# The last stage of a decoder trunk: spreading a per-token factor from its column instead of a diagonal, in another order, with stores from two engines

## The chip, the cores and the metric

The kernel runs on one core of a Trainium2 chip. The metric is the device time of one execution in microseconds. A core has five engines that run side by side and meet by semaphores: TensorE (PE; its weight loads are listed as PEld), VectorE (DVE), ScalarE (ACT), GpSimd (POOL) and SyncE (SP). Each takes its own instructions in the order of the program. Transfers between the chip's memory and a core's on-chip memory are started by an engine's queue and carried out by 16 DMA engines.

## The reference

One layer of a hybrid decoder trunk on 264 tokens (256 of a prompt and 8 of a sample), with 2048 features, in float32. After three gated branches and an output projection comes a channel mixer and then the final norm; only the end matters here:

```python
hid = jnp.square(jax.nn.relu(rms_norm(x, g_mlp) @ w_up))
x = x + hid @ w_down                     # 8192 -> 2048
...
y = xf * lax.rsqrt(jnp.mean(xf * xf, axis=-1, keepdims=True) + EPS) * g_final   # rms_norm(x, g_final)
```

The last norm needs, for each token, the sum of the squares of all its 2048 features; no output element can be finished before the last column of `hid @ w_down` is in that sum.

## The kernel before, in words

**Up to the tail.** Features lie on the 128 partitions, tokens along them, so a tensor `X` of 2048 features by 264 tokens is 16 tiles of 128 x 264. Weights come in chunks of 1 MB pairs and are split in two float32r parts, so that each product is three matmuls (lines 192 to 194). A table of chunks (`weight_plan`) sets the order; the work of the other engines is fitted in by a small planner with credits per engine. It ends with the loop over the chunks at line 1023. What follows, from line 1026 on, is written out by hand: the order of the calls is the order in which each engine takes its instructions, and semaphores are added for what depends on what.

**The tail.** Of the last product, 12 of the 16 feature tiles (`KA`) are complete by then and lie in `X`, already scaled by -0.5 times `g_final`, with the sum of their squares, element by element over tiles, in `sq2`. The last 512 features lack only the last four of the 64 contraction tiles. These four are computed the other way round: tokens on the partitions, features along them. For that the 264 tokens are cut into three groups of 128, 96 and 40 (`CUT`). For each group g:

- `half_mm(g, h)`: 12 matmuls (four contraction tiles by three parts) into one PSUM bank, for half h of the 512 features (line 1041). TensorE takes the halves in the order (0,0), (0,1), (1,0), (1,1), (2,0), (2,1).
- `other(g)`: the sum over features of `sq2`, by a matmul with a column of ones, into column g of the PSUM tile `inv` (line 1044). `other_in` reads it and adds the epsilon (line 1054).
- `half_sum(g, h)`: adds the residual on VectorE (line 1058), takes the squares and their sum on ScalarE (line 1062), and weighs by `g_final` on GpSimd (line 1066).
- `mean` twice on VectorE (line 1072): adds the sums of the two halves and the other features, over 2048. The result m stands in column 4 of the small tile `stat`, one row for each token.
- `seed` on ScalarE (line 1069): a first value s of 1/sqrt(m), from a table. One Newton step makes it exact: s (m s s - 3), times the -0.5 in the weights. `stat` column 5 is m s s (line 1078), column 6 the factor (line 1083, `root`).
- `token_out(g)`: scales the group's rows of 512 features by column 6 on ScalarE (line 1088) and stores them to `t_dram` (line 1089).
- The other 12 tiles have the tokens along the partitions, so the factor is needed there as a row, the same in all 128 partitions. `root_diag(g)` makes a diagonal matrix of the factors: the unit matrix times s on ScalarE (line 1077), then (-3 + m s s) times that on VectorE (line 1079). `spread_mm(g)` multiplies it by a matrix of ones: ones as the stationary operand, the diagonal as the moving one (line 1048). This gives the factors along the row in every partition.
- `piece(g, a, b)`: tiles a to b of `X` times that row, on VectorE from PSUM, or on GpSimd from a copy that ScalarE makes (`factor_copy`, line 1092), and a store to `y_dram` (lines 1099 and 1102).

All stores are issued by SyncE, in the order of the calls. The program ends when the last has landed.

Of the kernel before, what the change touches and what calls it, by code (L numbers as in the profile page):

```python
# [12 lines left out]
AF = mybir.ActivationFunctionType  # L13
ALU = mybir.AluOpType
AX = mybir.AxisListType

P = 128
# [3 lines left out]
N = TP + TS  # L21
# [37 lines left out]
PAD = 288  # L59
# [32 lines left out]
def hybrid_step(ctx: ExitStack, tc: tile.TileContext, head_in, x_in, par_in, st_in, row_in, wall, y_out, t_out, st_out):  # L92
    nc = tc.nc
# [34 lines left out]
    def acc():  # L128
        return psum.tile([P, 512], F32, name="acc", tag="acc")

    Gf = G.rearrange("p a n -> p (a n)")
# [82 lines left out]
    def later(n, fn):  # L214
        delayed.append((now[0] + n, fn))
# [263 lines left out]
    def lru_tail():  # L479
# [45 lines left out]
        stage("lru", "act", 0.52, [lambda ct=ct: decay(ct) for ct in range(8)])  # L525
        stage("lru", "pool", 0.2, [reset])
        stage("lru", "act", 0.65, [lambda c=c: root(c) for c in c4])
        stage("lru", "dve", 0.75, [lambda c=c: wide(c, TM, TM) for c in c4], 0)
        stage("lru", "dve", 0.43, [lambda c=c: a_of(c) for c in c4], 0)
# [329 lines left out]
    T = {}  # L859

    def end_tiles():
        e = [cpool.tile([P, 8, N], F32, name=f"end{i}", tag=f"B{i}").rearrange("p a n -> p (a n)") for i in range(4)]
        T["held"] = e[0][:, :4 * PAD].rearrange("p (m n) -> p m n", m=4)
        T["turned"] = e[1][:, :4 * PAD].rearrange("p (m n) -> p m n", m=4)
        T["resid"], T["sum"] = (t[:, :3 * 512].rearrange("p (g n) -> p g n", g=3) for t in e[2:])
        T["unit"], T["eye"] = (e[0][:, 4 * PAD + i * P:4 * PAD + (i + 1) * P] for i in range(2))
        T["minus"] = e[1][:, 4 * PAD + 24 + N:4 * PAD + 24 + N + P]
        nc.gpsimd.memset(T["minus"], -3.0)  # L868
        T["g"] = e[0][:, 4 * PAD + 2 * P:4 * PAD + 2 * P + 512]
        T["stat"] = e[1][:, 4 * PAD:4 * PAD + 24].rearrange("p (k g) -> p k g", g=3)  # L870
        T["copy"] = e[1][:, 4 * PAD + 24:4 * PAD + 24 + N]
        nc.gpsimd.memset(T["held"][:, :, N:], 0.0)
        nc.gpsimd.memset(T["unit"], 1.0)
        nc.gpsimd.affine_select(out=T["eye"], in_=T["unit"], pattern=[[1, P]], compare_op=ALU.is_equal, fill=0.0,
                                base=0, channel_multiplier=-1)
        nc.sync.dma_start(T["g"], row_in)
        later(2, lambda: nc.scalar.activation(T["g"], T["g"], AF.Copy, scale=-0.5))
# [79 lines left out]
    for i, ch in enumerate(chunks):  # L957
# [18 lines left out]
        if kind == "dense":  # L976
            rhs, fn = group(gi)
            n = groups[gi][2] // 2
# [3 lines left out]
            if c == 0:  # L982
                pss = [acc() for _ in range(4)] if gi > 2 else pair[4 * gi - 4:4 * gi]
                if groups[gi][:2] == ("w_down", 48) and groups[gi][3] == 3:
                    end_tiles()
# [40 lines left out]
    nL = len(chunks)  # L1026
    V, U = T["sum"], first[:, :3 * 512].rearrange("p (g n) -> p g n", g=3)
    Y = raw.rearrange("p a c -> p (a c)")
    stat, inv, fb, diag = T["stat"], acc(), [], []
    size = [b - a for a, b in zip(CUT, CUT[1:])]  # L1030

    def toks(g):
        return slice(CUT[g], CUT[g + 1])

    def token_mm(g, ps, a, b, steps):
        for s in steps:
            kt, way = divmod(s, 3)
            slot, at = (nL - 2 + kt // 2) % NHI, kt % 2 * 512
            w = (wlo if way == 2 else whi)[:, slot, at + a:at + b]
            x = hid(3, KD - TAIL + kt)[way == 1]  # L1040
            nc.tensor.matmul(ps[:size[g], :b - a], x[:, toks(g)], sent(w), start=s == 0, stop=s == 3 * TAIL - 1)  # L1041

    def other(g):
        nc.tensor.matmul(inv[:size[g], g:g + 1], sq2[:, toks(g)], ones[:, 0:1], start=True, stop=True)

    def spread_mm(g):
        fb.append(acc())
        nc.tensor.matmul(fb[g][:, :size[g]], T["unit"][:size[g], :], diag[g], start=True, stop=True)  # L1048

    def st_col(k, g):  # L1050
        return stat[:size[g], k, g:g + 1]

    def other_in(a, b):
        nc.vector.tensor_scalar(stat[:size[a], 0, a:b], inv[:size[a], a:b], EPS, None, op0=ALU.add)

    def token_sum(g, ps, a, b):
        n = size[g]
        nc.vector.tensor_tensor(halves(V[:n, g, a:b]), halves(T["resid"][:n, g, a:b]),
                                ps[:n, :b - a].rearrange("p (j t) -> p t j", t=2), op=ALU.add)

    def token_square(g, a, b, k):
        nc.scalar.activation(Gf[:size[g], a:b], V[:size[g], g, a:b], AF.Square, accum_out=st_col(k, g))

    def weighed(g, a, b):
        n = size[g]
        nc.gpsimd.tensor_tensor(U[:n, g, a:b], V[:n, g, a:b], T["g"][:n, a:b], op=ALU.mult)

    def seed(g, k, more):
        nc.scalar.activation(st_col(3, g), st_col(k, g), AF.Abs_reciprocal_sqrt, bias=st_col(more, g), scale=1.0 / D)  # L1069

    def mean(g, k, more, to):
        nc.vector.tensor_scalar(st_col(to, g), st_col(k, g), 1.0 / D, st_col(more, g), op0=ALU.mult, op1=ALU.add)

    def root_diag(g):
        n, y = size[g], st_col(3, g)
        seeded, d = (Gf[:n, (4 + 4 * i) * N + P * g:(4 + 4 * i) * N + P * g + n] for i in range(2))
        nc.scalar.activation(seeded, T["eye"][:n, :n], AF.Copy, scale=y)  # L1077
        nc.vector.scalar_tensor_tensor(st_col(5, g), st_col(4, g), y, y, op0=ALU.mult, op1=ALU.mult)
        nc.vector.scalar_tensor_tensor(d, T["minus"][:n, :n], st_col(5, g), seeded, op0=ALU.add, op1=ALU.mult)  # L1079
        diag.append(d)  # L1080

    def root(g):
        nc.vector.scalar_tensor_tensor(st_col(6, g), st_col(5, g), -3.0, st_col(3, g), op0=ALU.add, op1=ALU.mult)

    def token_out(g):
        n = size[g]
        y = Y[:n, KA * N + 512 * g:KA * N + 512 * (g + 1)]
        nc.scalar.activation(y, U[:n, g, :], AF.Copy, scale=st_col(6, g))
        nc.sync.dma_start(t_out[toks(g), :], y)

    def factor_copy(g):
        nc.scalar.copy(T["copy"][:, toks(g)], fb[g][:, :size[g]])

    def piece(g, a, b, own=False):
        n = size[g]
        at = KA * CUT[g]
        y = Y[:, at + a * n:at + b * n]
        by = T["copy"][:, toks(g)] if own else fb[g][:, :n]
        (nc.gpsimd if own else nc.vector).tensor_tensor(  # L1099
            y.rearrange("p (k n) -> p k n", n=n), X[:, a:b, toks(g)],  # L1100
            by[:, None, :].to_broadcast([P, b - a, n]), op=ALU.mult)
        send = lambda: nc.sync.dma_start(y_out[:, at + a * n:at + b * n], y)
        return send if own else send()

    every = range(3 * TAIL)
    bank = [[acc(), acc()] for _ in range(2)]

    def half_mm(g, h, steps=every):
        token_mm(g, bank[g][h], 256 * h, 256 * h + 256, steps)

    def half_sum(g, h):
        token_sum(g, bank[g][h], 256 * h, 256 * h + 256)
        token_square(g, 256 * h, 256 * h + 256, 1 + 6 * h)
        weighed(g, 256 * h, 256 * h + 256)

    def close(g):
        seed(g, 7, 2)
        mean(g, 7, 2, 4)
        root_diag(g)

    nc.vector.memset(inv[:, 0:3], 0.0)
    half_mm(0, 0)
    half_mm(0, 1)
    other(0)
    half_mm(1, 0)
    other(1)
    other(2)
    half_mm(1, 1, every[:5])
    half_sum(0, 0)
    half_sum(0, 1)  # L1130
    other_in(0, 1)
    mean(0, 1, 0, 2)
    close(0)
    spread_mm(0)
    half_mm(1, 1, every[5:])
    root(0)
    other_in(1, 3)
    token_out(0)
    half_sum(1, 0)
    piece(0, 0, 4)  # L1140
    factor_copy(0)
    send = piece(0, 8, 12, True)
    half_sum(1, 1)
    piece(0, 4, 8)
    send()
    bank.append([acc(), acc()])
    half_mm(2, 0)
    half_sum(2, 0)
    mean(1, 1, 0, 2)
    close(1)  # L1150
    half_mm(2, 1)
    spread_mm(1)
    half_sum(2, 1)
    piece(1, 0, 4)
    root(1)
    mean(2, 1, 0, 2)
    close(2)
    factor_copy(1)
    token_out(1)
    send = piece(1, 9, 12, True)  # L1160
    spread_mm(2)
    root(2)
    piece(1, 4, 9)
    send()
    token_out(2)
    piece(2, 0, 6)
    piece(2, 6, 12)


def _vec(a):  # L1170
# [95 lines left out]
```

## Time and profile before

| what | us |
|---|---|
| median of 3 runs (1302.89 to 1303.65) | 1303.21 |
| the profiled execution | 1303.09 |
| its span, first to last instruction | 1301.4 |
| TensorE busy | 1290.4 |
| VectorE busy | 838.2 |
| ScalarE busy | 722.0 |
| GpSimd busy | 113.3 |
| first matmul of the tail starts at | 1281.55 |
| last matmul of `half_mm(2, 1)` starts at | 1291.60 |
| last product on VectorE starts at | 1296.01 |
| last store is issued at | 1297.83 |

A row of the timeline has the start in us from the span's start, the duration in us, the engine, the line of the kernel, the operation, what is written and read, the shapes, the count, and in brackets how long the engine was idle before and whom it waited for. `end` is the tile that holds `stat`, the residual, the sums, the unit matrix and the copy; `acc` is any PSUM tile; `G` is a scratch tile with the diagonals; `raw` holds the finished output; `first` the weighed rows. SPq, DVEq and the like are an engine's sequencer. A matmul's duration overlaps the next one's. A float32 matmul in `other` or `spread_mm` shows as two instructions of each kind. In the table of windows the columns are the window, its length, the busy time and count of instructions of PE, PEld, DVE, ACT and POOL, the granted clock of TensorE, the share of the 16 DMA engines' time, and GB/s.

### The profile page before, as it was taken

Reading aid. Unit: us, or ns where it says so; the run is one execution under the profiler, and the core shown is the slowest. Engines: PE = TensorE matmul, PEld = TensorE weight load, DVE = VectorE, ACT = ScalarE, POOL = GpSimd, SP = SyncE. Lnnn points to the kernel's source line nnn. Section 1 sums busy time; section 2 is a strip of 40 time slices with the busy share of each in tenths; the row PEclk is TensorE's granted clock in tenths of the full one; section 3 lists DMA queues with packets and bytes.
Section 4 is the critical chain, followed back from the end, with each engine's and each line's share of the span. In section 5 each row is a group of like instructions: output and inputs, shape, how many; then the busy total and the mean of one; then the engine's idle time right before and its main releaser. Section 6 shows DMA issues by size and latency. Waiting matters only on the chain.

```text
span 1301.4 us, 26869 instructions
## 1 busy us (share of the span) xinstructions
PE 1290.4 (99%) x11458; PEld 1289.3 (99%) x11458; DVE 838.2 (64%) x1076; ACT 722.0 (55%) x1036; POOL 113.3 (9%) x154
## 2 busy tenths in 40 slices
PE   9999999999999999999999999999999999999996
PEld 9999999999999999999999999999999999999996
DVE  7886898776776677666555545554555554555554
ACT  7767677667674655455544334543345533455454
POOL 0250010110102023131000000000000000000023
PEclk9999999999999999999999999999999999999999
DMA  9655556555575564656555555555555555555661
GB/s 353 211 180 200 196 201 205 197 196 198 197 228 194 179 212 163 232 184 207 197 196 195 195 195 194 195 195 194 194 195 194 195 194 195 194 195 194 206 208 68
DMA packets 44361, 257.76 MB, mean 198 GB/s; under 512 B 9162, under 2 KB 10186, under 8 KB 15314
## 3 DMA queue, kind: packets, MB, share of 16 engines
q1 hardware_dynamic: 44242, 256.06, 58.2%
q8 instruction: 89, 1.46, 0.4%
q14 instruction: 30, 0.25, 0.1%
HBM read 252.29 MB, written 3.21 MB: 196 GB/s over the span
## 4 chain that ended last, share of the span: by engine, by line
PE 98%; DMA 0%; DVE 0%; ACT 0%; issue 0%; SPq 0%; DVEq 0%; ACTq 0%
PE acc L194 32%; PE acc L192 32%; PE acc L193 32%; PE acc L935 1%; PE acc L1041 0%; DMA first<-head_dram 0%; DVE raw L1099 0%; PE acc L1048 0%; SPq L158 0%; ACT end L1069 0%; ACT G L1077 0%; DVE G L1079 0%; ACT whi L169 0%; ACT A L291 0%; PE acc L266 0%
## 5 line engine op out<-in xcount | busy, mean ns | idle before, releaser
L170 DVE TENSOR_TENSOR wlo<-raw,whi 128x1024 fp32r<-128x1024 f32 (+1 forms) x479 | 586.8, 1227 | 440.6 <-ACT whi L169 434.9
L169 ACT CAST whi<-raw 128x1024 fp32r<-128x1024 f32 (+1 forms) x479 | 493.6, 1033 | 526.7 <-PE acc L193 475.1
L194 PE MATMUL acc<-A,wlo 128*128 128x264 f32 x1952 | 539.7, 276 | 0.0
L192 PE MATMUL acc<-A,whi 128*128 128x264 f32 x1952 | 539.7, 276 | 0.0
L193 PE MATMUL acc<-A,whi 128*128 128x264 f32 x1952 | 539.6, 276 | 0.0
L194 PEld LDWEIGHTS acc<-A,wlo 128*128 128x128 f32 x1952 | 369.5, 189 | 0.0
L192 PEld LDWEIGHTS acc<-A,whi 128*128 128x128 f32 x1952 | 369.5, 189 | 0.0
L193 PEld LDWEIGHTS acc<-A,whi 128*128 128x128 f32 x1952 | 369.5, 189 | 0.0
L194 PE MATMUL acc<-xn,wlo 128*128 128x264 f32 x1024 | 283.1, 276 | 0.0
L193 PE MATMUL acc<-xn,whi 128*128 128x264 f32 x1024 | 283.1, 276 | 0.0
L192 PE MATMUL acc<-xn,whi 128*128 128x264 f32 x1024 | 283.1, 276 | 0.0
L194 PEld LDWEIGHTS acc<-xn,wlo 128*128 128x128 f32 x1024 | 193.9, 189 | 0.0
L192 PEld LDWEIGHTS acc<-xn,whi 128*128 128x128 f32 x1024 | 193.8, 189 | 0.0
L193 PEld LDWEIGHTS acc<-xn,whi 128*128 128x128 f32 x1024 | 193.8, 189 | 0.0
L193 PE MATMUL acc<-Q,whi 128*128 128x264 f32 x628 | 173.6, 276 | 0.0
L192 PE MATMUL acc<-LH,whi 128*128 128x264 f32 x624 | 172.5, 276 | 0.0
L194 PE MATMUL acc<-LH,wlo 128*128 128x264 f32 x624 | 172.5, 276 | 0.0
L193 PEld LDWEIGHTS acc<-Q,whi 128*128 128x128 f32 x628 | 118.9, 189 | 0.0
L192 PEld LDWEIGHTS acc<-LH,whi 128*128 128x128 f32 x624 | 118.1, 189 | 0.0
L194 PEld LDWEIGHTS acc<-LH,wlo 128*128 128x128 f32 x624 | 118.1, 189 | 0.0
L583 ACT ACTIVATE G<-tmp,par 128x256 f32<-128x256 f32 x120 | 54.1, 498 | 2.9 <-DVE G L586 2.1
L868 POOL MEMSET end<- 128x128 f32 x1 | 0.2, 204 | 598.3 <-PE acc L194 598.3
(206 smaller groups left out, 871.7 us busy)
## 6 DMA issues: line engine op xcount, KB each, us to landing
raw<-wall_dram SPq DMA_DIRECT2D x226, 1024.0 KB, 4.9
raw<-wall_dram SPq DMA_DIRECT2D x18, 512.0 KB, 5.6
raw<-wall_dram SPq DMA_DIRECT2D x5, 256.0 KB, 3.3
X<-x_dram SPq DMA_DIRECT2D x4, 264.0 KB, 8.7
so_dram<-st SPq DMA_DIRECT2D x1, 1018.0 KB, 9.5
st<-st_dram SPq DMA_DIRECT2D x1, 912.0 KB
y_dram<-raw SPq DMA_DIRECT2D x3, 256.0 KB, 2.1
X<-x_dram SPq DMA_DIRECT2D x1, 528.0 KB
```

What stands on the lines that cost most here:

```text
L169: nc.scalar.copy(h[:, s], r)
L170: nc.vector.tensor_tensor(lo[:, s], r, f(h[:, s]), op=ALU.subtract)
L192: nc.tensor.matmul(ps[:, :N], whi_t, xh, start=first, stop=False)
L193: nc.tensor.matmul(ps[:, :N], whi_t, xl, start=False, stop=False)
L194: nc.tensor.matmul(ps[:, :N], wlo_t, xh, start=False, stop=last)
L583: nc.scalar.activation(dst[:, ct, :TP], vext[:, ct, k:k + TP], AF.Copy, scale=par[:, w:w + 1])
L868: nc.gpsimd.memset(T["minus"], -3.0)
L935: nc.tensor.matmul(pair[m][:, :N], w[:, m * P:(m + 1) * P], sent(A[:, x, :]), start=start and k == 0, stop=False)
```

## The change

**The spread.** The diagonal is gone, with the constant -3 matrix `T["minus"]` and its memset. `root_diag` becomes `root`, which computes columns 5 and 6 of `stat` only. `spread_mm` now takes column 6 itself, repeated 128 times by a step of zero, as the stationary operand, and the unit matrix as the moving one; the product is the same row in every partition.

**The order.** The first group's part up to `close(0)` now stands ahead of `half_mm(1, 0)`, `other(1)` and `other(2)`; `spread_mm(0)` comes after four steps of `half_mm(1, 1)` instead of five. `other_in(1, 3)` is behind the first piece of group 0. Group 1's first `mean` and its `seed` stand ahead of `half_sum(2, 0)`, and its `token_out(1)` right after its `root`.

**The stores.** `token_out` of groups 0 and 2 is issued by ScalarE, that of group 1 by SyncE. Group 1's GpSimd piece is stored by ScalarE. Group 2's product is one piece of 12 tiles with one store instead of two of six.

```diff
-        T["minus"] = e[1][:, 4 * PAD + 24 + N:4 * PAD + 24 + N + P]
-        nc.gpsimd.memset(T["minus"], -3.0)
...
     def spread_mm(g):
         fb.append(acc())
-        nc.tensor.matmul(fb[g][:, :size[g]], T["unit"][:size[g], :], diag[g], start=True, stop=True)
+        nc.tensor.matmul(fb[g][:, :size[g]], st_col(6, g).to_broadcast([size[g], P]), T["eye"][:size[g], :size[g]],
+                         start=True, stop=True)
...
-    def root_diag(g):
-        n, y = size[g], st_col(3, g)
-        seeded, d = (Gf[:n, (4 + 4 * i) * N + P * g:(4 + 4 * i) * N + P * g + n] for i in range(2))
-        nc.scalar.activation(seeded, T["eye"][:n, :n], AF.Copy, scale=y)
+    def root(g):
+        y = st_col(3, g)
         nc.vector.scalar_tensor_tensor(st_col(5, g), st_col(4, g), y, y, op0=ALU.mult, op1=ALU.mult)
-        nc.vector.scalar_tensor_tensor(d, T["minus"][:n, :n], st_col(5, g), seeded, op0=ALU.add, op1=ALU.mult)
-        diag.append(d)
-
-    def root(g):
-        nc.vector.scalar_tensor_tensor(st_col(6, g), st_col(5, g), -3.0, st_col(3, g), op0=ALU.add, op1=ALU.mult)
+        nc.vector.scalar_tensor_tensor(st_col(6, g), st_col(5, g), -3.0, y, op0=ALU.add, op1=ALU.mult)
...
-        nc.sync.dma_start(t_out[toks(g), :], y)
+        (nc.sync if g == 1 else nc.scalar).dma_start(t_out[toks(g), :], y)
...
-        send = lambda: nc.sync.dma_start(y_out[:, at + a * n:at + b * n], y)
-        return send if own else send()
+        return lambda queue: queue.dma_start(y_out[:, at + a * n:at + b * n], y)
...
     def close(g):
         seed(g, 7, 2)
         mean(g, 7, 2, 4)
-        root_diag(g)
+        root(g)
...
     half_mm(0, 1)
     other(0)
-    half_mm(1, 0)
-    other(1)
-    other(2)
-    half_mm(1, 1, every[:5])
     half_sum(0, 0)
     half_sum(0, 1)
     other_in(0, 1)
     mean(0, 1, 0, 2)
     close(0)
+    half_mm(1, 0)
+    other(1)
+    other(2)
+    half_mm(1, 1, every[:4])
     spread_mm(0)
-    half_mm(1, 1, every[5:])
-    root(0)
-    other_in(1, 3)
+    half_mm(1, 1, every[4:])
     token_out(0)
     half_sum(1, 0)
-    piece(0, 0, 4)
+    piece(0, 0, 4)(nc.sync)
+    other_in(1, 3)
     factor_copy(0)
     send = piece(0, 8, 12, True)
     half_sum(1, 1)
-    piece(0, 4, 8)
-    send()
+    piece(0, 4, 8)(nc.sync)
+    send(nc.sync)
     bank.append([acc(), acc()])
     half_mm(2, 0)
+    mean(1, 1, 0, 2)
+    seed(1, 7, 2)
     half_sum(2, 0)
-    mean(1, 1, 0, 2)
-    close(1)
+    mean(1, 7, 2, 4)
+    root(1)
+    token_out(1)
     half_mm(2, 1)
     spread_mm(1)
     half_sum(2, 1)
-    piece(1, 0, 4)
-    root(1)
+    piece(1, 0, 4)(nc.sync)
     mean(2, 1, 0, 2)
     close(2)
     factor_copy(1)
-    token_out(1)
     send = piece(1, 9, 12, True)
     spread_mm(2)
-    root(2)
-    piece(1, 4, 9)
-    send()
+    piece(1, 4, 9)(nc.sync)
     token_out(2)
-    piece(2, 0, 6)
-    piece(2, 6, 12)
+    send(nc.scalar)
+    piece(2, 0, 12)(nc.sync)
```

More of the change, by code (lines that the diff above doesn't have):

```diff
@@ L1028, in hybrid_step @@
     Y = raw.rearrange("p a c -> p (a c)")
-    stat, inv, fb, diag = T["stat"], acc(), [], []
+    stat, inv, fb = T["stat"], acc(), []
     size = [b - a for a, b in zip(CUT, CUT[1:])]
```

## The prediction

> **What bounds the kernel now.** I read the page first.
>
> ```profile
> span 1301.4 us, 26869 instructions
> PE 1290.4 (99%) x11458; PEld 1289.3 (99%) x11458; DVE 838.2 (64%) x1076; ACT 722.0 (55%) x1036; POOL 113.3 (9%) x154
> L868 POOL MEMSET end<- 128x128 f32 x1 | 0.2, 204 | 598.3 <-PE acc L194 598.3
> ```
>
> TensorE is full for all but some 11 us, and the diff touches nothing ahead of the tail except the removed memset: 0.2 us on an engine that stood idle for 598. So only the tail, from 1282 us on, can move. I read it next in the chain of waits in order of time, then instruction by instruction. TensorE, its weight load (PEld) and VectorE (DVE) in the first group:
>
> ```profile
> 1285.90 0.27 PE acc L1044 x4
> 1284.43 0.42 DVE L1058 TENSOR_TENSOR end<-end,acc 128x256 f32<-128x256 f32 x1 [0.92 <-PE acc L1041]
> 1286.19 0.16 DVE L1054 TENSOR_SCALAR end<-acc 128x1 f32<-128x1 f32 x1 [1.34 <-PE acc L1044]
> 1286.46 0.21 DVE L1072 TENSOR_SCALAR end<-end 128x1 f32<-128x1 f32 x1
> 1286.78 0.21 DVE L1072 TENSOR_SCALAR end<-end 128x1 f32<-128x1 f32 x1
> 1287.11 0.22 DVE L1078 SCALAR_TENSOR_TENSOR end<-end 128x1 f32<-128x1 f32 x1
> 1287.53 0.35 DVE L1079 SCALAR_TENSOR_TENSOR G<-end,G 128x128 f32<-128x128 f32 x1 [0.20 <-ACT G L1077]
> 1287.80 0.15 DVE L1083 SCALAR_TENSOR_TENSOR end<-end 128x1 f32<-128x1 f32 x1
> 1286.60 0.27 PE L1041 MATMUL acc<-whi,Q 128*96 128x256 f32 x1
> 1288.00 0.19 PEld L1048 LDWEIGHTS acc<-G,end 128*128 128x128 f32 x1 [1.34 <-issue]
> 1288.03 0.46 PE L1048 MATMUL acc<-G,end 128*128 128x128 f32 x2 [1.15 <-DVE end L1054]
> 1289.09 0.27 PE L1041 MATMUL acc<-whi,LH 128*40 128x256 f32 x1
> ```
>
> L1054 reads the first group's other sums, but waits until the last of the three groups' L1044 matmuls ends at 1286.17; DVE had been free since 1284.85. Five operations later TensorE, after its fifth step of half_mm(1,1) at 1286.60, has stood still 1.15 us for the spreading matmul. The group behind it, and the last, with ScalarE (ACT) and GpSimd (POOL):
>
> ```profile
> 1285.21 0.19 ACT L1062 ACTIVATION_READ_ACCUMULATOR G<-end 128x1 f32 x1
> 1286.77 0.29 ACT L1069 ACTIVATE end<-end 128x1 f32<-128x1 f32 x1 [1.37 <-DVE end L1072]
> 1287.10 0.40 ACT L1077 ACTIVATE G<-end,end 128x128 f32<-128x128 f32 x1
> 1288.05 0.72 ACT L1088 ACTIVATE raw<-first,end 128x512 f32<-128x512 f32 x1 [0.55 <-DVE end L1054]
> 1288.68 0.40 ACT L1062 ACTIVATE G<-end 96x256 f32<-96x256 f32 x1
> 1289.25 0.27 ACT L1092 COPY end<-acc 128x128 f32<-128x128 f32 x1
> 1289.59 1.28 POOL L1099 TENSOR_TENSOR raw<-X,end 128x512 f32<-128x512 f32 x1 [0.44 <-ACT end L1092]
> 1290.83 0.73 POOL L1066 TENSOR_TENSOR first<-end,end 96x256 f32<-96x256 f32 x1
> 1294.98 0.83 POOL L1099 TENSOR_TENSOR raw<-X,end 128x288 f32<-128x288 f32 x1 [1.18 <-ACT end L1092]
> 1290.60 0.41 DVE L1058 TENSOR_TENSOR end<-end,acc 40x256 f32<-40x256 f32 x1 [0.30 <-PE acc L1041]
> 1291.83 0.42 DVE L1078 SCALAR_TENSOR_TENSOR end<-end 96x1 f32<-96x1 f32 x1 [0.38 <-ACT end L1069]
> 1291.60 0.27 PE L1041 MATMUL acc<-wlo,LH 128*40 128x256 f32 x1
> 1292.82 0.43 PE L1048 MATMUL acc<-G,end 96*128 96x96 f32 x2 [0.95 <-DVE G L1079]
> 1293.29 0.55 DVE L1099 TENSOR_TENSOR raw<-X,acc 128x384 f32<-128x384 f32 x1 [0.29 <-PE acc L1048]
> 1295.06 0.64 DVE L1099 TENSOR_TENSOR raw<-X,acc 128x480 f32<-128x480 f32 x1
> 1296.01 0.40 DVE L1099 TENSOR_TENSOR raw<-X,acc 128x240 f32<-128x240 f32 x1
> ```
>
> Group 1's factor starts only after group 2's first sums (1290.60) and reaches TensorE at 1292.82. From 1293.29 DVE is nearly full to 1296.41, its last product. Then the stores, all on SyncE (SP), and the rate of the DMA engines:
>
> ```profile
> 1295.55 0.35 SPq L1089 DMA_DIRECT2D t_dram<-raw  x1
> 1297.39 0.34 SPq L1102 DMA_DIRECT2D y_dram<-raw  x1
> 1297.83 0.41 SPq L1102 DMA_DIRECT2D y_dram<-raw  x1
> 1296.20:1296.60 0.40, 0.00 (x0) 0.00 (x0) 0.21 (x1) 0.00 (x0) 0.00 (x0) 0.50 0.45 133
> 1297.40:1297.80 0.40, 0.00 (x0) 0.00 (x0) 0.00 (x0) 0.00 (x0) 0.00 (x0) 0.50 0.94 359
> 1296.60:1299.40 2.80, 0.00 (x0) 0.00 (x0) 0.00 (x0) 0.00 (x0) 0.00 (x0) 0.50 0.89 304
> 4.09 0.67 SPq L152 DMA_DIRECT2D raw<-wall_dram  x1
> ```
>
> The last two columns of the windows are DMA share and GB/s. Six stores leave SP from 1295.55 to 1297.83, one each 0.46 us; the last goes 1.42 us after DVE had made its data. The span ends 1301.4 - 1297.83 = 3.57 us after that issue.
>
> **The change part by part.** Spacings first, all from the rows above. A DVE operation that needs the one before starts 0.11 us after its end (1286.67 to 1286.78); one that doesn't, 0.08 before it (1287.88 to 1287.80). DVE to weight load is 0.12 (1287.88 to 1288.00), DVE to ACT 0.10, steps of TensorE 0.11.
>
> *First group.* Moved ahead of other(1) and other(2), L1054 waits only for its own sum and starts at 1284.8. The mean follows at 1285.05 to 1285.26, the seed on ACT at 1285.35 to 1285.64, the second mean after the accumulator read (1285.40) at 1285.45 to 1285.66. Removed are the scaled eye on ACT (0.40) and the 128x128 product (0.35); root remains: 0.22, then, now dependent, 0.15: 1285.77 to 1285.99 and 1286.10 to 1286.25. The weight load can start at 1286.37. TensorE comes to it after four steps, in the slot at 1286.60, its load 0.11 before: no stall, with 0.12 to spare. The eight remaining steps bring half_mm(2,0) to 1286.60 + 0.21 + 0.88 = 1287.70 where it was 1289.09: **1.39 us**. L1054 is now a read that other(1) may have to wait for; it is over at 1284.95, and other(1), with half_mm(1,1) and all later steps behind it, has its turn at 1285.74. DVE takes group 1's first sums at 1286.18 instead of 1287.94, the first product at 1287.09 to 1287.78 and, moved behind that, the other sums of groups 1 and 2 at 1287.71: in time for the mean at 1288.85.
>
> *The new stationary operand.* No row loads one column repeated. The nearest loads 128 columns in 0.19, twice per spread; I take that, since as many columns are loaded. Bounds: nothing at all (-0.19), and a load as long as the matmul pair, 0.46 (+0.27), per spread.
>
> *Group 1.* Its first mean and seed move ahead of group 2's sums; only the second mean and root stay behind. Sums at 1290.60 - 1.39 = 1289.21 to 1289.62, mean 1289.56 to 1289.77, root 1289.88 to 1290.36, matmul 1290.51. From sums to matmul that is 1.30 against 2.22: another **0.92**. TensorE, through with half_mm(2,1) by then (1291.60 - 1.39 = 1290.21 plus 0.27), waits no more. Hidden beside it on ACT: the first rows' output at 1286.34 to 1287.06, its store's issue, squares (0.40 and the read) to 1287.95, copy to 1288.17, squares to 1288.93, seed 1289.14 to 1289.42, 0.46 us ahead of root. On POOL: the 1.28 piece from 1288.25, the weighing to 1290.21, just ahead of the output at 1290.45 that needs it. That output, now ahead of group 2's second squares on ACT, ends at 1291.17; those squares end at 1291.65, and the mean that needs them starts at 1291.79, so 0.14 us later it would cost. Were L1078's 0.42 (seen once) the price instead of 0.22, each group's chain would be 0.2 longer.
>
> *Group 2.* The piece at 1291.00 to 1291.55 (0.55), means to 1291.99, seed to 1292.06, root to 1292.59, piece 1292.52 to 1293.16 (0.64), and the last, 480 elements in one, again 0.64: 1293.23 to 1293.87. DVE ended at 1296.41: 2.54 in all, so **0.23** more.
>
> *Stores.* An issue on ACT isn't in the trace: SP's take 0.34 to 0.41, at most 0.67 alone, and below that nothing, if it goes beside ACT's work; I take 0.36. The first stands in ACT's queue ahead of group 1's squares, the copy and thereby POOL (its 0.41 with the wait is in the times above). Group 1's rows, moved ahead of its first piece on SP, leave at 1291.20, the piece (ready at 1291.55) at 1291.64: nothing lost. At the end the last rows go from ACT at 1293.45, the POOL piece (0.83, done at 1293.13) at 1293.81, and behind these ACT has nothing more to do; on SP the two DVE pieces go at 1293.20 and 1293.91. The last issue moves from 1297.83 to 1293.91, 3.92 earlier: **1.38** more than DVE, the backlog gone.
>
> But data now bind. Before, data began 0.85 after the first issue (133 GB/s in the slice from 1296.20 puts it at 1296.4) and 896 KiB (by their shapes 192 + 240 + 144 + 80 + 120 + 120) = 918 KB at 304 GB/s lasted 3.02, to 1299.45; 1.95 later the span was over. After, 240 + 80 + 144 + 240 = 704 KiB = 721 KB from 1293.20 + 0.85 = 1294.05, at 304 to 359 GB/s: to 1296.42 or 1296.06, and the span ends at 1298.0 to 1298.4, not the 1297.5 of the issue alone. Gain 3.0 to 3.4; I take 3.25, as SP's gaps lowered the 304. The Trainium skill ("DMA: Bandwidth & Descriptors", section "Issuing engines are not separate DMA queues") says that stores from several engines run on the same 16 DMA engines and save only issue time. By it the end is 1298.2, without it 1297.5; the share of 0.89 under a single queue is on its side.
>
> Sum: 1.39 + 0.92 + 0.23 + 1.38 = 3.92, less 0.67 for data = 3.25. The profiled execution took 1303.09, the median is 1303.21; so 1299.84 to 1299.96: **1299.9**.
>
> **The rivals.** *The early read gains nothing:* if L1054 waits for all writes to that PSUM tile, however late they are placed, root ends at 1287.59, the matmul is at 1287.74 instead of 1286.60 and everything shifts by about 1.1: 1301.0. For it: it does wait today for columns it doesn't read. Against: it stands behind them in program order today.
>
> *The small chain is longer than its rows:* root at 0.42 in three groups and the repeated column at its upper bound are 3 x (0.20 + 0.27), less the 0.12 that TensorE has spare: 1.3 us, 1301.2. For it: the one 0.42 row; against: 0.21 and 0.22 in the others.
>
> *Slower: ACT held by its own stores.* All that stands behind an issue on ACT waits X for it. From the end of the first issue, 1287.11 + X, squares, copy, 1.28 on POOL, weighing, group 1's output, squares, seed, root and output take 5.73 us; then t and the POOL piece go, X apart: the last issue is at 1292.84 + 2X. With 3.57 behind it that is 1301.4 at X = 2.5, from where the kernel gets slower; at X = 4 it is 1304.4, or 1306.1 as a time. Against it: SP's rows, all under 0.7. The Trainium skill ("TensorE: Matmul & The Clock Gate", section "Architectural detail: the array is 16× 32×32, not 1× 128×128") calls ACT's queue a strict FIFO, so an issue would hold what is behind it; no run here shows it yet.
>
> **How the numbers follow.** Forecast 0.78, the early read 0.06, the long chain 0.08, ACT held 0.05, and 0.03 for no gain, or a loss, for a reason that I don't see. 0.2%, 2.6 us, is about what a measurement of this kernel tells from none. The forecast's own range is 1299.0 to 1300.8: 0.4 either way for the data rate, below it up to 0.5 for cheaper loads, above it the same for one 0.42 and loads somewhat dearer. Faster ends at 1300.6, so 0.04 of the forecast falls outside: faster 0.74. Within 0.2% are those 0.04, both smaller gains, and 0.04 of the last two cases: 0.22. Slower is what is left of these, 0.04: an X over 3.8, or the unseen. The range, to take in both smaller gains, is 1298.6 to 1301.5.
>
> **What would show it.** L1054 near 1284.8 without its 1.34 wait; no TensorE gap before the first spread; group 1's spread near 1290.5; DVE's last product near 1293.9; last issue on SP within 0.1 of it; ACT issues of 0.3 to 0.4; DMA share near 0.9 from 1294.1 to 1296.2. Wrong would be: L1054 still ending at 1286.3, weight loads over 0.3, or ACT gaps above 0.7 behind a store.

## The result, and the profile after

| | us |
|---|---|
| after, median of 15 runs (1299.91 to 1300.77) | 1300.39 |
| before, median of 15 runs beside them (1302.57 to 1303.65) | 1303.10 |
| ratio, with its 95% interval | 0.9979 (0.9971 to 0.9987) |
| forecast; range | 1299.9; 1298.6 to 1301.5 |

The change gains 2.71 us where 3.25 were forecast: sign and range held, and most of the size. Two things behind the number are off, by 0.89 us one way and 0.41 the other, so the errors partly cancel. First the page of the kernel after.

```profile
span 1298.8 us, 26855 instructions
PE 1290.4 (99%) x11458; PEld 1289.5 (99%) x11458; DVE 838.4 (65%) x1072; ACT 721.2 (56%) x1033; POOL 113.1 (9%) x153
```

TensorE's work is the same 1290.4 us; only what lies around it moved. The timeline of the kernel after, TensorE, its weight load and VectorE in the first group:

```profile
1284.60 0.42 DVE L1057 TENSOR_TENSOR end<-end,acc 128x256 f32<-128x256 f32 x1 [0.92 <-PE acc L1039]
1284.94 0.15 DVE L1053 TENSOR_SCALAR end<-acc 128x1 f32<-128x1 f32 x1
1286.18 0.16 DVE L1076 SCALAR_TENSOR_TENSOR end<-end 128x1 f32<-128x1 f32 x1
1286.67 0.19 PEld L1046 LDWEIGHTS acc<-end,end 128*128 128x128 f32 x1
1286.77 0.28 PE L1046 MATMUL acc<-end,end 128*128 128x128 f32 x1
1287.87 0.27 PE L1039 MATMUL acc<-whi,LH 128*40 128x256 f32 x1
```

L1053, the read of the other sums, no longer has a wait. The spread comes at 1286.77 with no idle time in front of it, and `half_mm(2, 0)` starts at 1287.87. The start of the tail differs by a few tenths from one profiled execution to the next (this one is 0.17 late: 1284.60 against 1284.43 for the same sum), so below all times of a tail are counted from the start of that sum. By this count `half_mm(2, 0)` moved from 4.66 to 3.27: 1.39 earlier, the number of the prediction.

The same timeline in groups 1 and 2, VectorE and then GpSimd:

```profile
1289.38 0.41 DVE L1057 TENSOR_TENSOR end<-end,acc 40x256 f32<-40x256 f32 x1 [0.17 <-PE acc L1039]
1290.03 0.32 DVE L1075 SCALAR_TENSOR_TENSOR end<-end 96x1 f32<-96x1 f32 x1
1290.39 0.65 DVE L1076 SCALAR_TENSOR_TENSOR end<-end 96x1 f32<-96x1 f32 x1
1291.18 0.43 PE L1046 MATMUL acc<-end,end 96*128 96x96 f32 x2 [0.53 <-DVE end L1076]
1292.99 0.72 DVE L1076 SCALAR_TENSOR_TENSOR end<-end 40x1 f32<-40x1 f32 x1
1294.27 0.66 DVE L1092 TENSOR_TENSOR raw<-X,acc 128x480 f32<-128x480 f32 x1
1289.61 0.73 POOL L1065 TENSOR_TENSOR first<-end,end 96x256 f32<-96x256 f32 x1
1290.30 0.72 POOL L1065 TENSOR_TENSOR first<-end,end 40x256 f32<-40x256 f32 x1
1292.91 0.79 POOL L1092 TENSOR_TENSOR raw<-X,end 128x288 f32<-128x288 f32 x1 [0.74 <-ACT end L1085]
```

Here is what the forecast missed. L1076, one number per partition, takes 0.16 in group 0, but 0.65 in group 1 and 0.72 in group 2. Compare its ends with GpSimd's: group 1's ends at 1291.04, GpSimd's weighing at 1291.02; group 2's at 1293.71, GpSimd's piece at 1293.70. L1075 of group 1 ends at 1290.35, with the weighing before that at 1290.34. In group 0 GpSimd was idle.

The stores after, on ScalarE's and SyncE's sequencers, and four windows with the DMA engines' share and GB/s in the last two columns:

```profile
1287.19 0.39 ACTq L1082 DMA_DIRECT2D t_dram<-raw  x1
1294.56 0.55 ACTq L1082 DMA_DIRECT2D t_dram<-raw  x1
1295.20 0.36 ACTq L1095 DMA_DIRECT2D y_dram<-raw  x1
1294.30 0.33 SPq L1095 DMA_DIRECT2D y_dram<-raw  x1
1291.88 0.35 SPq L1082 DMA_DIRECT2D t_dram<-raw  x1
1287.63 0.42 ACT L1061 ACTIVATE G<-end 96x256 f32<-96x256 f32 x1 [0.47 <-ACT raw L1081]
...
1295.00:1295.20 0.20, 0.00 (x0) 0.00 (x0) 0.00 (x0) 0.00 (x0) 0.00 (x0) 1.00 0.27 96
1295.40:1297.00 1.60, 0.00 (x0) 0.00 (x0) 0.00 (x0) 0.00 (x0) 0.00 (x0) 0.64 1.00 359
1297.00:1297.40 0.40, 0.00 (x0) 0.00 (x0) 0.00 (x0) 0.00 (x0) 0.00 (x0) 0.50 0.32 112
1297.40:1298.80 1.40, 0.00 (x0) 0.00 (x0) 0.00 (x0) 0.00 (x0) 0.00 (x0) 0.50 0.00 0
```

Data flow from about 1295.15 (a share of 0.27 in the slice to 1295.20), with the DMA engines full up to 1297.00. From there to 1297.40 the share is 0.32; counted as full time, the data would end at about 1297.13. Behind 1297.40 the span has 1.4 us more without data.

### The profile page after: what moved, and what is told of

It reads as the page before. It is cut to its first block, busy times and chain, and to the rows that moved or that the text cites. A ratio compares the mean times of both kernels' runs of the same rounds, so it can differ in the third digit from the quotient of the medians.

```text
span 1298.8 us, 26855 instructions
## 1 busy us (share of the span) xinstructions
PE 1290.4 (99%) x11458; PEld 1289.5 (99%) x11458; DVE 838.4 (65%) x1072; ACT 721.2 (56%) x1033; POOL 113.1 (9%) x153
## 3 DMA queue, kind: packets, MB, share of 16 engines
q8 instruction: 89, 1.46, 0.4%
## 4 chain that ended last, share of the span: by engine, by line
PE 99%; DMA 0%; DVE 0%; ACT 0%; issue 0%; SPq 0%; DVEq 0%; ACTq 0%
PE acc L193 32%; PE acc L194 32%; PE acc L192 32%; PE acc L933 1%; PE acc L1039 1%; DMA first<-head_dram 0%; DVE raw L1092 0%; DVE end L1076 0%; SPq L158 0%; PE acc L1046 0%; DVE end L1075 0%; ACT whi L169 0%; ACT A L291 0%; PE acc L266 0%; PE acc L1042 0%
```

## The experiments

| kernel | what differs | us | before beside it | ratio (95%) |
|---|---|---|---|---|
| e1 | after; root with one tensor operand | 1299.34 | 1303.06 | 0.9972 (0.9960 to 0.9983) |
| e2 | after; GpSimd off group 1's root | 1299.77 | 1303.06 | 0.9975 (0.9965 to 0.9985) |
| e12 | after; GpSimd off group 2's root | 1299.68 | 1302.90 | 0.9976 (0.9967 to 0.9985) |
| e5 | after; early read undone | 1301.67 | 1303.02 | 0.9990 (0.9982 to 0.9999) |
| e6 | before; early read alone | 1301.16 | 1303.02 | 0.9986 (0.9977 to 0.9995) |
| e4 | after; diagonal back | 1300.60 | 1303.06 | 0.9981 (0.9972 to 0.9990) |
| e3 | after; all stores on SyncE | 1300.39 | 1303.06 | 0.9978 (0.9969 to 0.9987) |
| e7 | e1; all stores on SyncE | 1299.48 | 1303.02 | 0.9972 (0.9962 to 0.9983) |
| e10 | before; stores from two engines, last two merged | 1302.80 | 1303.02 | 0.9998 (0.9989 to 1.0007) |
| e11 | e1; copy ahead of group 1's piece | 1299.20 | 1302.90 | 0.9972 (0.9961 to 0.9982) |
| e13 | e11; VectorE four tiles, GpSimd four | 1299.26 | 1302.90 | 0.9972 (0.9962 to 0.9983) |
| e14 | e1; copy right behind that piece | 1298.93 | 1303.02 | 0.9969 (0.9957 to 0.9981) |

The intervals are those of the ratio to the kernel before. The medians of before lie within 0.2 us of one another, so a difference under 0.3 us between two rows is read as none unless the trace shows its place.

**Why L1075 and L1076 grow.** The theory: a VectorE operation that reads two tensors from SBUF, even of one column, is held while GpSimd is inside an operation that reads SBUF, and runs only when that ends (called a hold below). `scalar_tensor_tensor` has two such operands, `tensor_scalar` one tensor and per-partition scalars. The rival: the length comes from the chain of small dependent operations, or from other readers of the same tile, whatever GpSimd does. e1 leaves GpSimd as it is and changes only the form of the operation:

```diff
-        nc.vector.scalar_tensor_tensor(st_col(5, g), st_col(4, g), y, y, op0=ALU.mult, op1=ALU.mult)
-        nc.vector.scalar_tensor_tensor(st_col(6, g), st_col(5, g), -3.0, y, op0=ALU.add, op1=ALU.mult)
+        nc.vector.tensor_scalar(st_col(5, g), st_col(4, g), y, y, op0=ALU.mult, op1=ALU.mult)
+        nc.vector.tensor_scalar(st_col(6, g), st_col(5, g), -3.0, y, op0=ALU.add, op1=ALU.mult)
```

> The changed kernel with root's two operations written as tensor_scalar (one tensor stream, the seed as the per-token scalar) instead of scalar_tensor_tensor (two tensor streams). Theory A, VectorE waits for GpSimd: an operation of VectorE with two inputs in SBUF that comes while GpSimd is inside one of its own cannot run until that one ends (in the changed kernel 0.65 us to 1291.04 with GpSimd's weighing ending at 1291.02, 0.72 us to 1293.71 with its piece ending at 1293.70); one tensor stream isn't held. Then all six take 0.15 to 0.22, the two groups lose 0.6 and 0.56 us less, and the time falls by about 1.1 us from 1300.4 to 1299.3. Rival B, the length comes from elsewhere (the chain of dependent small operations, readers of the same tile): the same operations keep 0.65 and 0.72 and the time stays at 1300.4.

Timeline of e1, VectorE and GpSimd, and below the line of dots the marks by which its tail is measured further on:

```profile
1290.08 0.21 DVE L1076 TENSOR_SCALAR end<-end 96x1 f32<-96x1 f32 x1
1292.30 0.20 DVE L1076 TENSOR_SCALAR end<-end 40x1 f32<-40x1 f32 x1
1290.15 0.71 POOL L1065 TENSOR_TENSOR first<-end,end 40x256 f32<-40x256 f32 x1
1292.17 0.79 POOL L1092 TENSOR_TENSOR raw<-X,end 128x288 f32<-128x288 f32 x1 [0.51 <-ACT end L1085]
...
1284.35 0.42 DVE L1057 TENSOR_TENSOR end<-end,acc 128x256 f32<-128x256 f32 x1 [0.92 <-PE acc L1039]
1287.62 0.27 PE L1039 MATMUL acc<-whi,LH 128*40 128x256 f32 x1
1289.13 0.41 DVE L1057 TENSOR_TENSOR end<-end,acc 40x256 f32<-40x256 f32 x1
1290.44 0.43 PE L1046 MATMUL acc<-end,end 96*128 96x96 f32 x2
1293.07 0.66 DVE L1092 TENSOR_TENSOR raw<-X,acc 128x480 f32<-128x480 f32 x1
```

Both L1076 run inside GpSimd's operations and end well before them, in 0.20 and 0.21. The time falls by 1.05, from 1300.39 to 1299.34. e2 keeps the two tensor operands and moves GpSimd instead: group 2's rows are weighed once, at the second half, so GpSimd is idle in group 1's root.

```diff
-        weighed(g, 256 * h, 256 * h + 256)
+        if g < 2:
+            weighed(g, 256 * h, 256 * h + 256)
+        elif h:
+            weighed(g, 0, 512)
```

> The changed kernel, but GpSimd's weighing of group 2 is one operation over 512 features after the second sums, so GpSimd is idle while group 1's factor is made; root is as in the change. Theory A: group 1's second root operation falls from 0.65 to 0.16, its spread comes 0.5 earlier, near 1290.7; group 2's root operations are then held by the longer weighing and by the piece, together at least 0.7, so most of it is lost again: 1299.9 to 1300.6. Rival B: group 1's stays at 0.65, its spread at 1291.2, whatever GpSimd does.

e12 is the opposite half: GpSimd's piece of group 1 is moved earlier, away from group 2's root, and stored by SyncE.

```diff
     spread_mm(1)
+    factor_copy(1)
     half_sum(2, 1)
+    send = piece(1, 9, 12, True)
     piece(1, 0, 4)(nc.sync)
+    send(nc.sync)
...
-    factor_copy(1)
-    send = piece(1, 9, 12, True)
...
-    send(nc.scalar)
```

> The same move of the copy and the store, with root's two operations as in the change (scalar_tensor_tensor). Theory A: GpSimd's piece is over at about 1292.95 and no longer covers group 2's second root operation, which falls from 0.72 to 0.16, while group 1's, still under a weighing, keeps about 0.65: together with the smaller burst 0.5 to 0.9 us faster than the change, 1299.5 to 1299.9. Rival B, the length does not come from GpSimd: both keep 0.65 and 0.72, only the burst's 0.2 to 0.5 is gained, 1299.9 to 1300.2.

Timelines of e2 and, in the second fence, of e12; in each L1076 of group 1 (96x1) and of group 2 (40x1), and GpSimd:

```profile
1289.84 0.15 DVE L1076 SCALAR_TENSOR_TENSOR end<-end 96x1 f32<-96x1 f32 x1
1291.96 0.71 DVE L1076 SCALAR_TENSOR_TENSOR end<-end 40x1 f32<-40x1 f32 x1
1289.06 0.72 POOL L1065 TENSOR_TENSOR first<-end,end 96x256 f32<-96x256 f32 x1
1291.88 0.79 POOL L1092 TENSOR_TENSOR raw<-X,end 128x288 f32<-128x288 f32 x1
```

```profile
1290.39 0.64 DVE L1076 SCALAR_TENSOR_TENSOR end<-end 96x1 f32<-96x1 f32 x1
1293.35 0.15 DVE L1076 SCALAR_TENSOR_TENSOR end<-end 40x1 f32<-40x1 f32 x1
1290.30 0.72 POOL L1065 TENSOR_TENSOR first<-end,end 40x256 f32<-40x256 f32 x1
1292.12 0.79 POOL L1092 TENSOR_TENSOR raw<-X,end 128x288 f32<-128x288 f32 x1
```

Where GpSimd is out of the way the operation takes 0.15, where it isn't 0.71 or 0.64, and the two kernels have the short and the long one in opposite groups. e2 gains 0.62, a little more than was expected of it, and e12 0.71 against the kernel after (e12 has moved a store, too). The theory stands, the rival falls. The Trainium skill has the rule ("SBUF — State Buffer", section "Who interferes with whom"): a VectorE instruction with two SBUF inputs contends with a GpSimd instruction that reads SBUF; the port that they share is an exclusive lock, and the order of issue decides who waits. These traces agree, down to 0.02 us at the ends.

**The early read.** e5 undoes it in the kernel after, e6 makes only this move in the kernel before (with `every[:5]`).

```diff
+    half_mm(1, 0)
+    other(1)
+    other(2)
+    half_mm(1, 1, every[:4])
     half_sum(0, 0)
...
     close(0)
-    half_mm(1, 0)
-    other(1)
-    other(2)
-    half_mm(1, 1, every[:4])
```

> The changed kernel with one move undone: half_mm(1, 0), other(1), other(2) and four steps of half_mm(1, 1) stand again ahead of group 0's sums, so that the read of the first group's other sums comes behind all three groups' matmuls. If that read waits for whatever TensorE wrote into the PSUM tile before it in the order of the program, it starts at about 1286.3 instead of 1284.9, TensorE stalls about 1.1 us before the first spread and everything behind it shifts: 1301.2 to 1301.6 against 1300.4. Rival: it waits for its own column, and nothing changes.

> The kernel before with that one move alone: group 0's sums, read and factor (diagonal and all) ahead of half_mm(1, 0). The read starts at 1284.9, the diagonal is done at about 1286.5, TensorE doesn't stall before the first spread; the rest shifts by 1.0 to 1.4 with all its later waits unchanged: 1301.7 to 1302.1 against 1303.1. Rival: the gain is eaten by the stores' backlog on SyncE, and it is under 0.4.

Timeline of e5:

```profile
1285.95 0.16 DVE L1053 TENSOR_SCALAR end<-acc 128x1 f32<-128x1 f32 x1 [1.34 <-PE acc L1042]
1287.42 0.46 PE L1046 MATMUL acc<-end,end 128*128 128x128 f32 x2 [0.90 <-DVE end L1076]
```

The old wait of 1.34 is back, TensorE idles 0.90 ahead of the first spread, and the time is 1.28 longer. e6 alone gains 1.86; its last product on VectorE ends 1.40 earlier in the tail than before's (10.58 after the first sum instead of 11.98), and its span 1.58 earlier. The rest lies in the start of the tail, which varies between executions. Both times lie a little outside what was expected, on the side of a larger effect. So this one move carries between half (1.28) and two thirds (1.86) of the change, and at VectorE's end what the prediction gave it.

**The stationary operand.** e4 puts the diagonal back and keeps the new order and stores.

```diff
-        nc.tensor.matmul(fb[g][:, :size[g]], st_col(6, g).to_broadcast([size[g], P]), T["eye"][:size[g], :size[g]],
-                         start=True, stop=True)
+        nc.tensor.matmul(fb[g][:, :size[g]], T["unit"][:size[g], :], diag[g], start=True, stop=True)
...
+        nc.scalar.activation(seeded, T["eye"][:n, :n], AF.Copy, scale=y)
         nc.vector.scalar_tensor_tensor(st_col(5, g), st_col(4, g), y, y, op0=ALU.mult, op1=ALU.mult)
+        nc.vector.scalar_tensor_tensor(d, T["minus"][:n, :n], st_col(5, g), seeded, op0=ALU.add, op1=ALU.mult)
+        diag.append(d)
```

> The changed kernel with the diagonal spread put back (scaled unit matrix on ScalarE, product with it on VectorE, ones as stationary operand); order and stores as in the change. By the rows of the kernel before, group 0's chain is 0.3 to 0.4 longer and TensorE stalls by 0.2 to 0.3, group 1 waits for a product of 0.31 that Theory A holds behind GpSimd too, group 2 for the scaled matrix and a 0.25 product: 0.6 to 1.0 us slower, 1301.0 to 1301.4. Rival: the weight load of the one repeated column had cost what the diagonal did, and the time stays at 1300.4.

1300.60: only 0.21 over the kernel after, where 0.6 to 1.0 were expected. Timeline of e4, VectorE and GpSimd:

```profile
1290.15 0.60 DVE L1078 SCALAR_TENSOR_TENSOR end<-end 96x1 f32<-96x1 f32 x1
1290.85 0.68 DVE L1079 SCALAR_TENSOR_TENSOR G<-end,G 96x96 f32<-96x96 f32 x1
1293.60 0.25 DVE L1079 SCALAR_TENSOR_TENSOR G<-end,G 40x40 f32<-40x40 f32 x1
1290.70 0.72 POOL L1066 TENSOR_TENSOR first<-end,end 40x256 f32<-40x256 f32 x1
1293.76 0.82 POOL L1097 TENSOR_TENSOR raw<-X,end 128x288 f32<-128x288 f32 x1 [1.03 <-ACT end L1090]
```

In e4 group 1's root is held, but group 2's isn't: its product starts at 1293.60, ahead of GpSimd's piece at 1293.76, which comes 1.03 us after GpSimd fell idle. Without the diagonal the copy and so the piece came at 1292.91, early enough to hold group 2's L1076 for half a microsecond. So the shorter root seems to have been paid for with a hold. That this is the whole of the missing gain is argued from these rows, not shown; a diagonal whose operations have one tensor operand wasn't tried. The repeated column itself costs nothing: its weight load is 0.19, as the ones' was.

**The stores.** e3 takes the second engine away from the kernel after, e7 from e1, with the same edit; e10 gives it to the kernel before.

```diff
-        (nc.sync if g == 1 else nc.scalar).dma_start(t_out[toks(g), :], y)
+        nc.sync.dma_start(t_out[toks(g), :], y)
...
-    send(nc.scalar)
+    send(nc.sync)
```

> The changed kernel with all stores issued by SyncE, in the same order of calls. Theory: with few stores left at the end a second queue saves only issue time: ScalarE's squares of group 1 come 0.4 earlier (nothing waits for them), the last issue goes from 1295.20 to about 1295.6, the DMA engines are full until 1297.1 in either case: 0 to 0.4 us slower, 1300.4 to 1300.8. Rival, the second queue is what took the backlog away: about 1 us slower, 1301.4.

> The changed kernel with the one-stream root and all stores on SyncE. With two queues the one-stream root took 1299.34. If the second queue is worth nothing here either: 1299.3 to 1299.5. Rival, now that the factors come 1.1 us earlier the issues crowd again: 1299.7 or more.

In e10, on the kernel before, the line `send()` is gone as well:

```diff
-        nc.sync.dma_start(t_out[toks(g), :], y)
+        (nc.sync if g == 1 else nc.scalar).dma_start(t_out[toks(g), :], y)
...
-    piece(2, 0, 6)
-    piece(2, 6, 12)
+    send(nc.scalar)
+    piece(2, 0, 12)
```

> The kernel before with the stores' part alone: the first and third group's rows and group 1's GpSimd piece stored by ScalarE, the last product and its store in one. VectorE ends as before, 12.0 us after the second sum starts; the last issue comes 0.2 to 0.4 after that instead of 1.42, and with the DMA engines as the limit the gain is 0.8 to 1.2: 1301.9 to 1302.3. Rival: as in the changed kernel, where one queue did as well as two, it is worth less than 0.3.

The sequencers' rows of e3, its store of group 2's rows and its last issue; then of e10, group 1's L1078 and GpSimd's weighing beside it:

```profile
1294.37 0.32 SPq L1082 DMA_DIRECT2D t_dram<-raw  x1
1295.21 0.38 SPq L1095 DMA_DIRECT2D y_dram<-raw  x1
```

```profile
1291.66 0.80 DVE L1078 SCALAR_TENSOR_TENSOR end<-end 96x1 f32<-96x1 f32 x1 [0.39 <-ACT end L1069]
1291.73 0.71 POOL L1066 TENSOR_TENSOR first<-end,end 40x256 f32<-40x256 f32 x1
```

e3 ran in 1300.39, exactly the kernel after. e7 is 0.14 behind e1, e10 0.22 ahead of before: nothing that can be told from none, though 0.8 to 1.2 were expected of e10. In e3 the last issue comes 10.85 us after the tail's first sum instead of 10.60, 0.25 later, and still the span ends at 14.24 instead of 14.20. Where the DMA engines are full (a share of 1.00 from 1295.40 on in the kernel after), earlier issues deliver the data hardly sooner. This is the rule of the Trainium skill that the prediction cited ("DMA: Bandwidth & Descriptors", section "Issuing engines are not separate DMA queues"), and e3 and e7 agree.

The equal times hide two small effects. From VectorE's last product to the end of the span it is 4.02 in e3 against 3.87 after, so the second engine is worth some 0.15 there (spans are given to 0.1). But ScalarE's first issue delays the copy for GpSimd, GpSimd's piece and the weighing behind it (5.01 after the first sum, 4.90 in e3), and the hold ends with the weighings: without this issue VectorE's last product ends at 10.22 in e3, 0.11 earlier than after.

In e10 this second effect is larger. The weighing comes 0.38 later in the tail than before's, L1078 is held for 0.80 instead of 0.42, until group 2's weighing is over as well, and VectorE ends at 12.22 instead of 11.98. The last issue, at 12.76, is 0.64 earlier than before's 13.40, but the first issue of the last burst of stores is 0.38 later (11.50 against 11.12), and the span ends at 16.94 against 16.97. So e10's time is no clean measure of what the stores alone are worth.

**A better version.** With GpSimd's piece no longer in anyone's way (e1), the copy that feeds it can go earlier. e11 is e1 with the same move as e12. e13 also gives GpSimd four of group 1's tiles and VectorE four instead of five:

```diff
-    send = piece(1, 9, 12, True)
+    send = piece(1, 8, 12, True)
...
-    piece(1, 4, 9)(nc.sync)
+    piece(1, 4, 8)(nc.sync)
```

> The one-stream root, and group 1's copy of the factor moved ahead of group 2's second sums on ScalarE, so that GpSimd makes its piece about 0.6 us earlier and SyncE stores it right behind the first piece, while the DMA engines are idle. The last burst has 560 KiB instead of 704 KiB, and ScalarE has one issue less at the end. If the end hangs on the last burst (issues and data), 0.2 to 0.5 us faster than the one-stream root alone: 1298.8 to 1299.1. Rival: it hangs on VectorE's last product and what follows it alone, and the time stays at 1299.3.

> As the one-stream root with the copy early, and GpSimd's piece of group 1 with four tiles instead of three, VectorE's second piece with four instead of five. VectorE's last product ends 0.1 us earlier and the last burst has 48 KiB less: 0.1 to 0.2 us faster than with three tiles. Rival: GpSimd's longer piece, 1.05 us instead of 0.8, delays nothing and the end doesn't move by more than 0.05.

Timeline of e11:

```profile
1291.43 0.21 ACT L1085 COPY end<-acc 128x96 f32<-128x96 f32 x1
1291.68 0.55 DVE L1092 TENSOR_TENSOR raw<-X,acc 128x384 f32<-128x384 f32 x1 [0.41 <-ACT end L1085]
```

The copy and VectorE's piece both only read the bank with the spread factor, yet the piece, which stands behind the copy in the program, waits 0.41 for it. VectorE's last product ends 9.74 after the first sum where e1 has 9.38, which eats most of the gain: 1299.20 and, with the tiles shifted as well, 1299.26, neither of which can be told from e1. e14 therefore puts the copy right behind that piece, ahead of group 2's means, and stores GpSimd's piece from SyncE ahead of VectorE's second piece:

```diff
     piece(1, 0, 4)(nc.sync)
-    mean(2, 1, 0, 2)
-    close(2)
     factor_copy(1)
     send = piece(1, 9, 12, True)
+    mean(2, 1, 0, 2)
+    close(2)
     spread_mm(2)
+    send(nc.sync)
     piece(1, 4, 9)(nc.sync)
     token_out(2)
-    send(nc.scalar)
```

> The one-stream root, with group 1's copy of the factor moved only so far that it still comes behind VectorE's first piece of the group (both read the same PSUM bank) but ahead of group 2's seed, and GpSimd's piece stored by SyncE ahead of VectorE's second piece. If ScalarE's copy had held VectorE's first piece in the run with the copy further ahead (0.41 us idle there), VectorE starts that piece as in the one-stream root alone, 6.6 us after group 0's second sum, and the smaller burst now shows: 1298.9 to 1299.2. Rival, the end hangs on VectorE's last product and a fixed 3.6 us: 1299.3 as with the one-stream root alone.

Timeline of e14:

```profile
1291.14 0.55 DVE L1092 TENSOR_TENSOR raw<-X,acc 128x384 f32<-128x384 f32 x1
```

The wait is gone, and e14 is the fastest of all: 1298.93 (1298.86 to 1299.18), 1.46 less than the kernel after and 4.09 less than before beside it. Of the 1.46, 1.05 are e1's; the other 0.41 aren't split between the copy's place and the store's.

## Why the prediction was right, and where it was wrong

The gain of the profiled tails can be split by the prediction's own terms, counted from the tail's first sum shown (1284.43, 1284.60, and 1284.35 in e1). VectorE's last product ends 11.98 us after it in the kernel before, 10.33 after, 9.38 in e1; the span ends at 16.97, 14.20 and 13.25.

| step | predicted | after | e1 |
|---|---|---|---|
| first group, early read | 1.39 | 1.39 | 1.39 |
| group 1, sums to spread | 0.92 | 0.42 | 0.91 |
| rest of group 1 and group 2 | 0.23 | -0.16 | 0.30 |
| end of VectorE to end of span | 0.71 | 1.12 | 1.12 |
| sum | 3.25 | 2.77 | 3.72 |

First row: the start of `half_mm(2, 0)`, 4.66 before, 3.27 in both others (e1: 1287.62 - 1284.35). Second: from group 2's first sum to group 1's spread, 2.22 before, 1291.18 - 1289.38 = 1.80 after, 1290.44 - 1289.13 = 1.31 in e1. Third: what is left to the end of VectorE's last product. Fourth: what is left of the span's end. The medians give 2.71 and 3.72 for the sums.

**First group: right,** in size and in mechanism. L1053 starts 0.34 after the sum and unhindered, the spread follows without a gap, and e5 and e6 confirm it from both sides. The rival by which the read gains nothing is out.

**The price of the spread: right.** The load is 0.19, neither end of the bounds.

**Group 1: the step that failed.** The prediction took root as 0.22 and then 0.15, "1289.88 to 1290.36". It started as forecast, 0.65 after group 2's first sums began where 0.67 was forecast, but took 0.32 and 0.65: from sums to spread 1.80 us instead of the 1.30, where e1 has 1.31. The 0.42 of before's L1078 was set aside as "seen once". It was the trace's one showing of the hold, and the row beside it tells. Timeline of the kernel before, the row not shown so far:

```profile
1291.53 0.71 POOL L1066 TENSOR_TENSOR first<-end,end 40x256 f32<-40x256 f32 x1
```

L1078 ran from 1291.83 to 1292.25, GpSimd's weighing to 1292.24. The other eight operations of root there met GpSimd idle, or within 0.08 us of an operation's start or end. The nearest to an exception is group 2's L1083: it takes 0.14 though GpSimd's piece is recorded as starting 0.01 us before it. It stands right behind a product that VectorE had begun before the piece, so the order of issue may have favoured VectorE; that wasn't tested. The prediction's timetable had GpSimd's weighing up to 1290.21 and noted only who needs its result, not who runs beside it; group 2's weighing, which follows at once and held L1076, isn't in it. The change moved root into these two operations. The rival "the small chain is longer than its rows" had the symptom, but not the size (0.20 more in each of three groups, where L1076 alone lost 0.50 and 0.57 in two), gave no cause for it, and took it together with a dear load, which didn't come.

**Group 2: the same step.** Here it is 0.72 for L1076 against 0.15. Without the hold the two rows are 0.91 and 0.30, against 0.92 and 0.23: the spacings were sound.

**The stores: nearly right, and mostly without the second engine.** The backlog between VectorE's end and the last issue fell from 1.42 to 0.27, by 1.15 where 1.38 was taken. From VectorE's end to the end of the span the kernel before has 4.99, e10 4.72, e3 4.02 and the kernel after 3.87. So 0.97 of the 1.12 in the table come with all stores on SyncE, and two engines and the merged store without the new order bring 0.27. What is left for most of it is the order, by which group 1's rows leave at 1291.88 instead of in the last burst. This is argued by what remains: the order was not run by itself.

**The data limit: right in kind, too dear by 0.41.** From the first issue of the last burst to the end of the span the prediction had 0.85, 2.0 to 2.4 for the data, and 1.95: 4.8 to 5.2 us. It took 4.5 (1294.30 to 1298.8). The windows have the data from 1295.15 to, counted as full time, 1297.13: 2.0 us, as taken for the faster rate of 359 GB/s; but behind it 1.7 pass, not 1.95. Why this last stretch is shorter stays open.

**ScalarE held by its stores: out as a slowdown.** The issues took 0.39, 0.55 and 0.36 where 0.36 was taken, and a loss would have begun at 2.5. Group 1's squares idled 0.47 behind the first; what that costs through GpSimd is the 0.11 of e3.

## What to carry to other kernels

Look along a timeline for what runs beside a short operation, not only for what it waits for: a duration may hold a wait. VectorE operations on the critical path that read two tensors from SBUF should be out of GpSimd's way or be rewritten with per-partition scalars, which here gained more (1.05 us) than the second store queue and the missing diagonal together (0.14 in e7 and 0.21 in e4). A second issuing engine was worth next to nothing here, where the transfers nearly filled the DMA engines anyway.

## What the runs showed of the hardware that was not expected

An operation on 96 numbers may last 0.65 us instead of 0.16, because of GpSimd (0.80 in e10, through two operations of GpSimd), and is listed as busy all the while, not as idle. A store of 40 rows took ScalarE's sequencer 0.55 (kernel after), SyncE's 0.32 (e3). Two reads of one PSUM bank, by ScalarE and VectorE, ran in the order of the program: 0.41 of waiting in e11, and the other way round in e3, where the copy waits for the piece:

```profile
1287.68 0.27 ACT L1085 COPY end<-acc 128x128 f32<-128x128 f32 x1 [0.36 <-DVE raw L1092]
```

Whether the chip would let them overlap was not tried.
